# Two attention stages of a whole-model kernel: TensorE's order fixed in the code, with padded last keys

## The chip, the cores and the metric

The kernel runs on one core of a Trainium2 chip. A core has TensorE (PE in the profile: matrix products and transposes; its weight loads are PEld), VectorE (DVE), ScalarE (ACT), GpSimd (POOL) and SyncE (SP, which issues transfers here). Each engine works through a queue of its own, in order; semaphores hold an instruction until what it reads is ready and what it overwrites has been read. The metric is device time in microseconds (us) of one execution. The kernel before takes 2580.34 us, the median of 3 runs (2580.19 to 2582.79).

## The reference

The program computes two whole transformer-like layers in float32 for 512 tokens of width 1024. The change lies in the mixer of the first block, which has 16 extra leading tokens ("meta", 528 in all) and two attentions of 8 heads of 64. Queries are taken in four blocks of 128; a block sees the meta tokens and all blocks up to its own. In the code heads go in pairs, so that there are 4 chunks of heads times 4 query blocks.

```python
def stick_breaking_attention(q, k, v):
    ...
        z = jnp.einsum('bhtd,bhsd->bhts', q[:, :, q0:q1], k[:, :, :q1]).astype(jnp.float32) * scale
        strict = jnp.arange(q1)[None, :] < jnp.arange(q0, q1)[:, None]
        log_1m = jnp.where(strict, jax.nn.log_sigmoid(-z), 0.0)
        csum = jnp.cumsum(log_1m, axis=-1)
        log_a = jax.nn.log_sigmoid(z) + csum[..., -1:] - csum
        a = jnp.where(strict, jnp.exp(log_a), 0.0)
        outs.append(jnp.einsum('bhts,bhsd->bhtd', a.astype(v.dtype), v[:, :, :q1]))
def latent_attention(q_nope, q_rope, k_nope, k_rope, v, cid):
    ...
        s = (jnp.einsum('bhtd,bhsd->bhts', q_nope[:, :, q0:q1], k_nope[:, :, :kend])
             + jnp.einsum('bhtd,bsd->bhts', q_rope[:, :, q0:q1], k_rope[:, :kend]))
        p = jax.nn.softmax(jnp.where(mask, s, NEG_INF), axis=-1)
        outs.append(jnp.einsum('bhts,bhsd->bhtd', p.astype(v.dtype), v[:, :, :kend]))
```

After them come `gate_sb * (y_sb @ w_sb_o) + gate_mla * (y_mla @ w_mla_o)` with sigmoid gates, and `@ w_out`.

## The kernel before

**Long products.** Every weight matrix is loaded in float32 tiles (`wraw`, two buffers), split by ACT into a rounded part `whi` (L286) and by DVE into the rest `wlo` (L287), three buffers each. A projection is then three products for every 128 rows of depth (L301: hi by xh, hi by xl, lo by xh) into a PSUM bank of the pool `l`. A product has 512 columns (`lin1`), or it goes as a pair of 256 and 272 columns into two banks (`lin2`, 528 tokens). In the two attention stages the pools are z=2 (scores), l=2, a=2 (transposes and attention outputs): `l` holds two banks, and whoever writes the third waits for the eviction of the first.

**`stick`, the stick-breaking attention.** For each chunk c: the projections of the next chunk's q (`sbq`, evicted by DVE at L683) and k (`sbk`, evicted in two halves by L247), four of the 16 gate projections (`gs`, `gm`), and for each query block b a short chain: scores on PE (both heads in one tile, L709, for 144 and 272 keys; one head at a time, L669, for 400 and 528), a mask product (L671, L711), on ACT Abs (L226), Exp and Ln (L236), on DVE `sp` (L723), a running sum `cs` (L727), `e` (L731, L733), and on ACT the last Exp. `attn_pv` then transposes the probabilities on PE (L634), copies them out of PSUM (`at`, L638; the last 16 keys, L640) and multiplies them by v (L645), two heads in the two halves of the columns; ACT and DVE store the result (`ysbh`, `ysbl`).

**`latent`, the softmax attention.** First v (`mlav`) is made by 30 long products (L757) of `uv`; then for each chunk q and k (`uq`, `uk`; copies by ACT, L243) and in chunks 0 and 2 the rotated part `t12`, which needs the table `rope` (a DMA at L748). The chain is a maximum on DVE (L800, L802), Exp with its sum on ACT (L236), reciprocal and scaling on DVE (L814, L816), and `attn_pv` as above. The 8 projections by `wo` of the stick result (96 products) stand in the code behind the loop. Behind the stage, `wo` of the latent result is multiplied by the gate on DVE, added to the other half on POOL (`gm`, L609) and split (`ooh`, `ool`) for `wout` (L328).

**What sets the order.** The framework orders the instructions of all engines by priorities and its own cost estimates. `attn_pv` and the weight splits stand in `high_priority(offset=100)`; so a short product goes in when the framework believes it ready, between any two long ones.

Of the kernel before, what the change touches and what calls it, by code (L numbers as in the profile page):

```python
# [215 lines left out]
class Kern:  # L216
# [301 lines left out]
    def mixer(self, n, h):  # L518
# [15 lines left out]
        with ExitStack() as stS:  # L534
            S = self.pool(stS, "S")
            vt = S.tile([P, 5, 512], F32, name="sbv")
            with ExitStack() as st:
# [53 lines left out]
            self.stick(S, x, n.rs, vt, ysb, masks[:, :P], gs, gm)  # L591
# [7 lines left out]
        with ExitStack() as st:  # L599
            self.latent(st, cq, ckv, kr, masks[:, P:], ymla, ysb, gs)  # L600
# [20 lines left out]
    def attn_pv(self, pool, probs, c, nb, vt, ydst, b):  # L621

        nc = self.nc
        hp = ExitStack()
        hp.enter_context(self.tc.high_priority(offset=100))
        slots = [(i, hh) for i in range(nb) for hh in range(2)] + [(nb, hh) for hh in range(2)]
        where = {}
        for g0 in range(0, len(slots), 4):
            grp = slots[g0:g0 + 4]
            pt = self.sbank()  # L630
            at = pool.tile([P, 512], F32, name="at", bufs=3)
            for j, (i, hh) in enumerate(grp):
                kk = P if i < nb else META
                nc.tensor.transpose(pt[:kk, j * P:(j + 1) * P], probs[hh][:, i * P:i * P + kk], self.ident)  # L634
                where[(i, hh)] = at[:kk, j * P:(j + 1) * P]
            n1 = sum(1 for i, hh in grp if i < nb)
            if n1:
                (nc.vector.tensor_copy if (g0 // 4) % 2 else nc.scalar.copy)(at[:, :n1 * P], pt[:, :n1 * P])  # L638
            if n1 < len(grp):
                nc.vector.tensor_copy(at[:META, n1 * P:len(grp) * P], pt[:META, n1 * P:len(grp) * P])  # L640
        po = self.sbank()[:, :P]
        for i in range(nb + 1):
            kk = P if i < nb else META
            for hh in range(2):
                nc.tensor.matmul(po[64 * hh:64 * hh + 64, :], vt[:kk, i, (2 * c + hh) * 64:(2 * c + hh + 1) * 64],  # L645
                                 where[(i, hh)], start=i == 0, stop=i == nb)
        sl = slice(b * P, (b + 1) * P)
        nc.scalar.copy(ydst[0][:, c, sl], po)
        self.tt(ydst[1][:, c, sl], po, ydst[0][:, c, sl], ALU.subtract)
        hp.close()  # L650

    def units(self):

        for b in range(4):
            n = META + (b + 1) * P
            for heads in (((0, 1),) if n <= 272 else ((0,), (1,))):
                z = self.psp["z"].tile([P, 2, 512], F32, name="z", tag="z")
                if n <= 512:
                    yield b, heads, n, z[:, :len(heads), :n], [[(z[:, i, :n], 0, n)] for i in range(len(heads))]
                else:  # L660
                    w = n // 2
                    yield b, heads, n, z[:, :, :w], [[(z[:, s, :w], s * w, (s + 1) * w) for s in range(2)]]

    def scores(self, pieces, q, k, mask):

        nc = self.nc
        for i, (ps, a, b) in enumerate(pieces):
            last = i == len(pieces) - 1
            nc.tensor.matmul(ps, q, k[:, a:b], start=True, stop=not last)  # L669
            if last:  # L670
                nc.tensor.matmul(ps[:, b - a - P:], self.idb, mask, start=False, stop=True)  # L671

    def stick(self, S, x, rs, vt, ysb, mask, gs, gm):
# [3 lines left out]
        qk = {}  # L677

        def proj(c):
            q = S.tile([P, T], F32, name="sbq", bufs=2)  # L680
            k = S.tile([P, TM], F32, name="sbk", bufs=2)
            ps = self.lin1(d["sbq"][c], x, KD, META)
            nc.vector.scalar_tensor_tensor(q, ps, 0.125, rs[:, META:], op0=mul, op1=mul)  # L683
            for p, a, b in self.lin2(d["sbk"][c], x, KD):
                self.tt(k[:, a:b], p, rs[:, a:b], mul)
            qk[c] = q, k

        def gates(i):
            for m in range(4 * i, 4 * i + 4):
                ps = self.lin1(d["gate"][m], x, KD, META)  # L690
                dst = (gs if m < KD else gm)[:, m % KD, :]
                self.tt(dst, ps, rs[:, META:], mul)
                nc.gpsimd.tensor_scalar(dst, dst, self.v("b_gate", m), 1.0, op0=add, op1=mul)

        proj(0)
        late = None
        for c in range(4):
            if c < 3:
                proj(c + 1)
            if c:  # L700
                gates(c - 1)
            q, k = qk[c]
            probs = {}
            for b, heads, n, z, pieces in self.units():
                nh = len(heads)
                if nh == 2:
                    for hh in heads:
                        r = slice(64 * hh, 64 * hh + 64)
# [657 lines left out]
```

## Time and profile before

| | us |
|---|---|
| median of 3 runs | 2580.34 |
| the profiled execution | 2579.18 |
| span of its trace | 2577.4 |
| `stick`, first score to last product by `sbv` | 171.7 (512.1 to 683.8) |
| end of `stick` (last gates) | 693.9 |
| `latent` with its `uv` and `wo`, to the first product of `ymh` | 112.4 (693.9 to 806.3) |

PE is busy for 98% of the span, DVE for 53%, ACT for 38%. The granted clock of TensorE is 0.996 of full speed on the mean. Times in the trace are from the span's start.

### The profile page before, as it was taken

The page shows a single profiled execution, that of the slowest core. Times are in us where ns is not written, and L with a number is a line of the kernel's source. Part 1 is how long each engine was busy: PE and PEld are TensorE (multiplying, and loading weights), DVE is VectorE, ACT ScalarE, POOL GpSimd, SP SyncE. Part 2 cuts the span into 40 slices and gives each one's busy share as a digit, 9 for nine tenths or more (in the row PEclk, how much of TensorE's full clock was granted, in tenths as well). Part 3 has the DMA queues.
Part 4 walks back from the last instruction along what each step waited for, and adds up shares of the span by engine and source line. Part 5 has one row for each costly group of instructions (what it writes and reads, how often), then busy time and mean ns, then how long its engine had stood idle before and what let it go on. Part 6 is the DMA issues. An engine that isn't in the chain of part 4 may idle for free.

```text
span 2577.4 us, 33167 instructions
## 1 busy us (share of the span) xinstructions
PE 2526.4 (98%) x13330; PEld 2087.8 (81%) x13334; DVE 1355.5 (53%) x2108; ACT 978.6 (38%) x1561; POOL 312.2 (12%) x250
## 2 busy tenths in 40 slices
PE   8999999999999999999999999999999899999999
PEld 8999997867767788888777788888888568888887
DVE  4324347355565542334678755355475755535544
ACT  4222234344563532223534633223344553322332
POOL 3101011011102120101100111001122111100110
PEclk9999999999999999999999999999999999999999
DMA  4222333211112423333323332332333213233232
GB/s 137 91 91 84 98 92 132 75 57 58 51 38 81 147 98 98 95 101 100 107 85 98 115 98 92 92 103 96 92 109 99 58 43 129 94 94 100 94 93 98
DMA packets 76339, 239.43 MB, mean 93 GB/s; under 512 B 9044, under 2 KB 11348, under 8 KB 75928
## 3 DMA queue, kind: packets, MB, share of 16 engines
q1 hardware_dynamic: 76184, 237.30, 29.2%
q8 instruction: 105, 1.72, 0.3%
q14 instruction: 50, 0.41, 0.1%
HBM read 225.72 MB, written 8.40 MB: 91 GB/s over the span
## 4 chain that ended last, share of the span: by engine, by line
PE 88%; DVE 5%; ACT 3%; issue 2%; POOL 1%; DMA 1%; SPq 0%; DVEq 0%; POOLq 0%; ACTq 0%
PE l L301 75%; PE l L328 3%; PE a L645 2%; PE z L669 1%; PE l L314 1%; PE a L634 1%; DVE h L247 1%; DVE xl L404 1%; PE s L1272 1%; PE a L382 1%; PE a L1294 0%; POOL gm L247 0%; DVE wlo L287 0%; PE a L1300 0%; ACT whi L286 0%
## 5 line engine op out<-in xcount | busy, mean ns | idle before, releaser
L286 ACT CAST whi<-wraw 128x1024 fp32r<-128x1024 f32 (+4 forms) x440 | 430.3, 979 | 1115.2 <-PE l L301 911.0
L301 PE MATMUL l<-xh,whi 128*128 128x512 f32 (+3 forms) x2368 | 785.5, 357 | 0.5 <-DVE sbk L247 0.5
L301 PE MATMUL l<-xh,wlo 128*128 128x512 f32 (+3 forms) x2368 | 780.9, 356 | 0.0
L301 PE MATMUL l<-xl,whi 128*128 128x512 f32 (+3 forms) x2368 | 780.7, 355 | 0.0
L287 DVE TENSOR_TENSOR wlo<-wraw,whi 128x1024 fp32r<-128x1024 f32 (+4 forms) x440 | 503.4, 1145 | 283.8 <-ACT whi L286 272.7
L301 PEld LDWEIGHTS l<-xh,whi 128*128 128x128 f32 (+1 forms) x2368 | 421.3, 188 | 66.1 <-issue 4.8
L301 PEld LDWEIGHTS l<-xh,wlo 128*128 128x128 f32 (+1 forms) x2368 | 420.7, 188 | 63.7 <-issue 1.9
L301 PEld LDWEIGHTS l<-xl,whi 128*128 128x128 f32 (+1 forms) x2368 | 421.5, 188 | 62.3 <-issue 2.1
L247 POOL TENSOR_TENSOR acc<-acc,sq 128x512 f32<-128x512 f32 (+1 forms) x63 | 99.9, 1586 | 471.1 <-ACT sq L226 434.2
L301 PE MATMUL l<-chh,whi 128*128 128x512 f32 x384 | 149.4, 389 | 0.0
L301 PE MATMUL l<-chl,whi 128*128 128x512 f32 x384 | 149.4, 389 | 0.0
L301 PE MATMUL l<-chh,wlo 128*128 128x512 f32 x384 | 149.4, 389 | 0.0
L247 POOL TENSOR_TENSOR t<-g,xrs 128x528 f32<-128x528 f32 (+1 forms) x44 | 75.8, 1724 | 563.8 <-ACT g L236 563.8
L301 PE MATMUL l<-hh,wlo 128*128 128x256 f32 (+2 forms) x528 | 140.1, 320 | 0.0
L301 PE MATMUL l<-hh,whi 128*128 128x256 f32 (+2 forms) x528 | 140.0, 319 | 0.0
L301 PE MATMUL l<-hl,whi 128*128 128x256 f32 (+2 forms) x528 | 139.8, 319 | 0.0
L247 POOL TENSOR_TENSOR cc<-cc,xrs 128x512 f32<-128x512 f32 x48 | 62.8, 1308 | 586.7 <-ACT cc L236 586.7
L247 DVE TENSOR_TENSOR t<-l,t 128x256 f32<-128x256 f32 (+1 forms) x66 | 32.3, 516 | 148.1 <-PE l L301 144.8
L247 DVE TENSOR_TENSOR g<-l,xrs 128x256 f32<-128x256 f32 (+1 forms) x66 | 32.3, 516 | 122.2 <-PE l L301 116.2
L301 PEld LDWEIGHTS l<-hh,whi 128*128 128x128 f32 x528 | 88.3, 188 | 6.9
L301 PEld LDWEIGHTS l<-hh,wlo 128*128 128x128 f32 x528 | 88.1, 188 | 6.9
L301 PEld LDWEIGHTS l<-hl,whi 128*128 128x128 f32 x528 | 88.1, 188 | 6.8
(342 smaller groups left out, 3202.9 us busy)
## 6 DMA issues: line engine op xcount, KB each, us to landing
wraw<-in_up SPq DMA_DIRECT2D x96, 512.0 KB, 3.4
wraw<-in_dn SPq DMA_DIRECT2D x64, 384.0 KB, 3.1
wraw<-in_ffn_g SPq DMA_DIRECT2D x44, 512.0 KB, 3.4
wraw<-in_ffn_u SPq DMA_DIRECT2D x44, 512.0 KB, 3.4
wraw<-in_ffn_d SPq DMA_DIRECT2D x32, 448.0 KB, 3.3
wraw<-in_hy SPq DMA_DIRECT2D x20, 512.0 KB, 3.4
wraw<-in_ffn_d SPq DMA_DIRECT2D x16, 512.0 KB, 3.5
wraw<-in_gate SPq DMA_DIRECT2D x16, 512.0 KB, 3.4
```

What stands on the lines that cost most here:

```text
L247: return (eng or self.nc.vector).tensor_tensor(out, a, b, op=op)
L286: nc.scalar.copy(hi, raw)
L287: nc.vector.tensor_tensor(lo, raw, hi, op=ALU.subtract)
L301: self.nc.tensor.matmul(ps, a[:, k * m:(k + 1) * m], b[:, k0 + k, c0:c1], start=first and k == 0 and pi == 0, stop=last and k == kc - 1 an ...
L314: self.nc.tensor.matmul(ps[:c1 - c0, :n], a[:, k, c0:c1], b[:, j * n:(j + 1) * n], start=k == 0 and pi == 0, stop=k == nk - 1 and pi == 2)
L328: self.nc.tensor.matmul(ps, a[:, k * P:(k + 1) * P], b[:, k, t0:t1], start=k == 0 and pi == 0, stop=k == kc - 1 and pi == 2)
L382: nc.tensor.matmul(p[:, c - a:c - a + w], r[:w, i:i + 1].to_broadcast([w, P]), self.ident[:w, :w], start=True, stop=True)
L404: nc.vector.scalar_tensor_tensor(n.x[1][:, k, :], hs[k], g, n.x[0][:, k, :], op0=ALU.mult, op1=ALU.subtract)
L634: nc.tensor.transpose(pt[:kk, j * P:(j + 1) * P], probs[hh][:, i * P:i * P + kk], self.ident)
L645: nc.tensor.matmul(po[64 * hh:64 * hh + 64, :], vt[:kk, i, (2 * c + hh) * 64:(2 * c + hh + 1) * 64], where[(i, hh)], start=i == 0, stop=i ...
L669: nc.tensor.matmul(ps, q, k[:, a:b], start=True, stop=not last)
L1272: nc.tensor.matmul(z[:, i * n:(i + 1) * n], qt[r, 2 * g + i, b * P:(b + 1) * P], kt[r, g, k0:k0 + n], start=False, stop=i == 1)
```

## The change

In both stages PE's order is now the order of the code (`by_hand`). A projection is a generator that yields after each step (a 512-column product, or a 256+272 pair), and `fill(n)` puts n steps between the short groups. The other engines are still ordered by the framework.

- `attn_pv` is split into `attn_t` (transposes, copies) and `attn_v` (the products by v, now one unbroken group of a block). The last 16 keys are copied into a `rest` tile of 128 rows whose other rows are zero, and v's last block is zeroed too, so that their product has 128 rows.
- The scores of the two heads of 400 and 528 keys are issued beside each other.
- Gates are spread 3, 4, 4, 5 over the chunks of `stick` (before: none, 4, 4, 4 and 4 behind the loop).
- In `latent`, `uq` and `uk` of chunk 0 stand ahead of the `uv` products, and `wo` of the stick result is spread 2, 1, 2, 3 over the chunks.
- Behind `latent`, the addition of `gm` and `gs` goes to DVE for m of 5 and more.

```diff
+    def by_hand(self):
+        return self.tc.manual_schedule(engines={mybir.EngineType.PE})
+    def step_lin(self, src, x, kc, done, c0=0, two=False):
+        hi, lo = self.wload(src, kc * P)
+        segs, ev = self.banks2() if two else self.banks1(c0)
+        for k in range(kc):
+            for pi, (a, b) in enumerate(((hi, x[0]), (hi, x[1]), (lo, x[0]))):
+                for ps, t0, t1 in segs:
+                    self.nc.tensor.matmul(ps, a[:, k * P:(k + 1) * P], b[:, k, t0:t1],
+                                          start=k == 0 and pi == 0, stop=k == kc - 1 and pi == 2)
+                yield
+        done(ev)
+    def fill(self, steps=None):
+        n = 0
+        while self.todo and (steps is None or n < steps):
+            if next(self.todo[0], self) is self:
+                self.todo.pop(0)
+            else:
+                n += 1
...
-            self.tt(gm[:, m, :], gm[:, m, :], gs[:, m, :], add, nc.gpsimd)
+            self.tt(gm[:, m, :], gm[:, m, :], gs[:, m, :], add, nc.gpsimd if m < 5 else None)
...
+    def last_keys(self, pt, o, probs, nb, rest, where):
+        for hh in range(2):
+            self.nc.tensor.transpose(pt[:META, o + hh * P:o + (hh + 1) * P], probs[hh][:, nb * P:nb * P + META], self.ident)
+            where[(nb, hh)] = rest[:, hh * P:(hh + 1) * P]
+        self.nc.vector.tensor_copy(rest[:META, :], pt[:META, o:o + 2 * P])
+    def attn_v(self, where, c, nb, vt, ydst, b):
...
+            po = self.sbank()[:, :P]
+            for i in range(nb + 1):
+                for hh in range(2):
+                    nc.tensor.matmul(po[64 * hh:64 * hh + 64, :], vt[:, i, (2 * c + hh) * 64:(2 * c + hh + 1) * 64],
+                                     where[(i, hh)], start=i == 0, stop=i == nb)
...
+    def scores(self, units, q, k, mask):
...
+        for row in zip(*todo):
+            for hh, (ps, a, b), last in row:
+                nc.tensor.matmul(ps, q(hh), k(hh)[:, a:b], start=True, stop=not last)
...
+            def qdone(ev):
+                nc.vector.scalar_tensor_tensor(q, ev[0][0], 0.125, rs[:, META:], op0=mul, op1=mul)
+            def kdone(ev):
+                for p, s in ev:
+                    self.tt(s(k), p, s(rs), mul)
+            yield from self.step_lin(d["sbq"][c], x, KD, qdone, META)
+            yield from self.step_lin(d["sbk"][c], x, KD, kdone, two=True)
...
+        for c in range(4):
+            ng = (3, 4, 4, 5)[c]
+            self.todo = ([proj(c + 1)] if c < 3 else []) + [gates.pop(0) for _ in range(ng)]
+            if c == 0:
+                self.fill(8)
+            probs = start(c, 0)
+            if late:
+                self.attn_v(*late)
+            self.fill(12)
+            for b in range(4):
+                if b < 3:
+                    nxt = start(c, b + 1)
+                    self.fill((14, 18, 22)[b])
+                else:
+                    self.fill(24 * ng + (48 if c < 3 else 0) - (8 if c == 0 else 0) - 102)
+                t = self.attn_t(S, probs, c, b + 1, vt, ysb, b, rest[b % 2])
+                self.fill(6)
+                if b < 3:
+                    self.attn_v(*t)
+                    self.fill(4)
+                    probs = nxt
+                else:
+                    late = t
+            self.fill()
+        self.attn_v(*late)
...
+        self.todo = [proj(0)]
+        self.fill()
+        w = self.wload(d["uv"][0], 1024)
...
+        late, m = None, 0
+        for c in range(4):
+            nm = (2, 1, 2, 3)[c]
+            self.todo = ([proj(c + 1)] if c < 3 else []) + [wo(m + i) for i in range(nm)]
+            m += nm
+            probs = start(c, 0)
+            if late:
+                self.attn_v(*late)
+            self.fill(6)
+            for b in range(4):
+                if b < 3:
+                    nxt = start(c, b + 1)
+                    self.fill(5)
+                t = self.attn_t(L, probs, c, b + 1, vt, ymla, b, rest[b % 2])
+                self.fill(4)
...
```

How the order moves, at three places. On PE in chunk 2 of `stick`, the products by v of the last block of chunk 1 (`sbv`) stand in the program before singly between long products:

```order
L301 MATMUL l<-xl,whi 128x512
L301 MATMUL l<-xh,wlo 128x512
L645 MATMUL a<-at,sbv 64x128
L301 MATMUL l<-xh,whi 128x512
L645 MATMUL a<-at,sbv 64x128
L301 MATMUL l<-xl,whi 128x512
L645 MATMUL a<-at,sbv 64x128
L301 MATMUL l<-xh,wlo 128x512
```

and in the changed one, at a block's end, together (`rest` is the padded tile):

```order
L712 MATMUL z<-masks,idb 128x128
L683 MATMUL a<-at,sbv 64x128 x8
L683 MATMUL a<-rest_4908,sbv 64x128 x2
L343 MATMUL l<-xh,whi 128x512
L343 MATMUL l<-xl,whi 128x512
```

Ten products by v stand in one group where they stood one by one between long ones.

On DVE, the evictions of the projections `sbq` and `sbk` of chunk 2 stand before between single operations of the block of 528 keys:

```order
L733 SCALAR_TENSOR_TENSOR e<-z,cs 128x528
L287 TENSOR_TENSOR wlo<-wraw,whi 128x1024
L683 SCALAR_TENSOR_TENSOR sbq<-l,xrs 128x512
L723 SCALAR_TENSOR_TENSOR sp<-z,e 128x528
L247 TENSOR_TENSOR sbk<-l,xrs 128x256
L727 SCALAR_TENSOR_TENSOR cs<-cst,sp 128x528
L733 SCALAR_TENSOR_TENSOR e<-z,cs 128x528
L247 TENSOR_TENSOR sbk<-l,xrs 128x272
```

and in the changed program, in chunk 1, behind the whole chain of the 272-key block and of the 400-key block:

```order
L762 SCALAR_TENSOR_TENSOR sp<-z,e 128x544
L766 SCALAR_TENSOR_TENSOR cs<-cst,sp 128x272 x2
L770 SCALAR_TENSOR_TENSOR e<-z,cs 128x272 x2
L734 SCALAR_TENSOR_TENSOR sbq<-l,xrs 128x512
L287 TENSOR_TENSOR wlo<-wraw,whi 128x1024
L674 COPY rest_4907<-a 16x256
L247 TENSOR_TENSOR ysbl<-a,ysbh 128x128
L762 SCALAR_TENSOR_TENSOR sp<-z,e 128x400 x2
L766 SCALAR_TENSOR_TENSOR cs<-cst,sp 128x400 x2
L772 SCALAR_TENSOR_TENSOR e<-z,cs 128x400 x2
L287 TENSOR_TENSOR wlo<-wraw,whi 128x1024
L247 TENSOR_TENSOR sbk<-l,xrs 128x256
```

Each eviction has moved from the middle of a chain to its end.

On ACT, the copies of q and k of the second chunk of `latent` stand before ahead of the Exps of the first two blocks (128x144, 128x272):

```order
L243 COPY q_6730<-l 64x512
L243 COPY q_6733<-l 64x512
L243 COPY k_6756<-l 64x256
L243 COPY k_6760<-l 64x256
L286 CAST whi<-wraw 128x384
L243 COPY k_6756<-l 64x272
L243 COPY k_6760<-l 64x272
L236 ACTIVATE e,sm<-z,sm 128x144 x2
L236 ACTIVATE e,sm<-z,sm 128x272 x2
```

and in the changed program behind them:

```order
L236 ACTIVATE e,sm<-z,sm 128x144 x2
L286 CAST whi<-wraw 128x512
L236 ACTIVATE e,sm<-z,sm 128x272 x2
L243 COPY q_6766<-l 64x512
L243 COPY q_6769<-l 64x512
L665 COPY at<-a 128x256
L286 CAST whi<-wraw 128x384
L243 COPY k_6807<-l 64x256
L243 COPY k_6807<-l 64x272
```

The copies have moved behind four Exps, and go head by head instead of half by half.

## Rows read from the trace of the kernel before

**Rows 1.** The page, part 1: engine, busy us, share of span, instructions.

```profile
PE 2526.4 (98%) x13330; PEld 2087.8 (81%) x13334; DVE 1355.5 (53%) x2108; ACT 978.6 (38%) x1561; POOL 312.2 (12%) x250
```

**Rows 2.** Busy time in two stretches (`latent`, `stick`), with clock, DMA share, GB/s.

```profile
693.90:806.30 112.40, 110.28 (x696) 78.50 (x695) 69.41 (x188) 63.40 (x160) 0.93 (x1) 1.00 0.14 41
512.10:683.80 171.70, 171.25 (x933) 117.83 (x934) 105.61 (x168) 82.43 (x149) 23.85 (x42) 1.00 0.16 54
```

**Rows 3.** What PE waited for, 495 to 807: total, times, longest.

```profile
PE l L301 <- ACT q L243: 1.3, 2, 0.7
```

**Rows 4.** Timeline of PE: start, duration, engine, line, operation; records (two a product).

```profile
545.57 0.43 PE L645 MATMUL a<-at,sbv 128*64 128x128 f32 x2
545.93 0.50 PE L301 MATMUL l<-xh,whi 128*128 128x512 f32 x1
546.37 0.43 PE L645 MATMUL a<-at,sbv 128*64 128x128 f32 x2
```

**Rows 5.** Timeline of PE, ten products by v in one group.

```profile
645.54 0.48 PE L301 MATMUL l<-xh,whi 128*128 128x512 f32 x1
645.95 1.46 PE L645 MATMUL a<-at,sbv 128*64 128x128 f32 x20
647.34 0.50 PE L301 MATMUL l<-xl,whi 128*128 128x512 f32 x1
647.68 0.39 PE L301 MATMUL l<-xh,wlo 128*128 128x512 f32 x1
647.91 0.39 PE L301 MATMUL l<-xh,whi 128*128 128x512 f32 x1
```

**Rows 6.** Timeline of PE, scores of two heads together and of one head.

```profile
656.99 0.73 PE L709 MATMUL z<-sbk,sbq 64*128 64x272 f32 x4
657.65 0.28 PE L711 MATMUL z<-masks,idb 128*128 128x128 bf16 x2
...
664.59 0.94 PE L669 MATMUL z<-sbk,sbq 64*128 64x400 f32 x2
665.46 0.23 PE L671 MATMUL z<-masks,idb 128*128 128x128 bf16 x1
```

**Rows 7.** Timeline of all engines: first and last of a 272-key chain.

```profile
658.42 0.61 ACT L226 ACTIVATE e<-z 128x544 f32<-128x544 f32 x1
...
663.19 0.48 DVE L731 SCALAR_TENSOR_TENSOR e<-z,cs 128x272 f32<-128x272 f32 x1
```

**Rows 8.** DVE by shape, 512 to 684: count, busy us, mean ns, idle before.

```profile
L287 DVE TENSOR_TENSOR wlo<-wraw,whi 128x1024 fp32r<-128x1024 f32 x19 | 23.6, 1244 | 5.1 <-ACT whi L286 5.0
...
L727 DVE TENSOR_TENSOR_SCAN cs<-cst,sp 128x400 f32<-128x400 f32 x8 | 7.9, 986 | 0.1
...
L733 DVE SCALAR_TENSOR_TENSOR e<-z,cs 128x400 f32<-128x400 f32 x8 | 5.1, 634 | 0.5
L723 DVE SCALAR_TENSOR_TENSOR sp<-z,e 128x400 f32<-128x400 f32 x8 | 4.6, 574 | 4.9 <-ACT e L236 4.9
...
L683 DVE SCALAR_TENSOR_TENSOR sbq<-l,xrs 128x512 f32<-128x512 f32 x2 | 1.4, 685 | 0.0
```

**Rows 9.** ACT by shape, 512 to 684.

```profile
L236 ACT ACTIVATE e<-e 128x400 f32<-128x400 f32 x24 | 12.3, 534 | 0.3
```

**Rows 10.** ACT by shape, 693 to 807.

```profile
L243 ACT COPY q<-l 64x512 f32<-64x512 f32 x8 | 4.6, 580 | 0.2 <-PE l L301 0.2
...
L236 ACT ACTIVATE e<-z,sm 128x272 f32<-128x272 f32 x8 | 3.8, 482 | 3.4 <-DVE sm L803 3.4
```

**Rows 11.** Transfers issued 688 to 696: count, KB, us from issue to landing.

```profile
rope<-in_rope SPq DMA_DIRECT2D x1, 528.0 KB, 3.6
```

**Rows 12.** Timeline of PE behind `latent`; in brackets, idle before and releaser.

```profile
835.74 0.78 PE L328 MATMUL l<-ooh,whi 128*128 128x512 f32 x1 [2.09 <-ACT ooh L291]
```

**Rows 13.** Timeline of POOL, the addition behind `latent`.

```profile
832.93 2.11 POOL L247 TENSOR_TENSOR gm<-gm,gs 128x512 f32<-128x512 f32 x1 [2.12 <-DVE gm L247]
```

**Rows 14.** Busy time right behind that wait of PE (columns of rows 2).

```profile
835.78:839.20 3.42, 3.42 (x8) 2.39 (x9) 2.36 (x3) 0.85 (x1) 2.11 (x1) 0.50 0.47 188
```

More of the change, by code (lines that the diff above doesn't have):

```diff
@@ L619, in mixer, with attn_t @@
         return h, upd
-    def attn_pv(self, pool, probs, c, nb, vt, ydst, b):
+    def attn_t(self, pool, probs, c, nb, vt, ydst, b, rest):
         nc = self.nc
-        hp = ExitStack()
-        hp.enter_context(self.tc.high_priority(offset=100))
-        slots = [(i, hh) for i in range(nb) for hh in range(2)] + [(nb, hh) for hh in range(2)]
+        slots = [(i, hh) for i in range(nb) for hh in range(2)]
         where = {}
[L628 to L662, printed above, removed]
@@ L664, in scores @@
-    def scores(self, pieces, q, k, mask):
-        nc = self.nc
[L667 to L671, printed above, removed]
+        with self.tc.high_priority(offset=100):
+            for g0 in range(0, len(slots), 4):
+                grp = slots[g0:g0 + 4]
+                pt = self.sbank()
+                at = pool.tile([P, 512], F32, name="at", bufs=3)
+                for j, (i, hh) in enumerate(grp):
+                    nc.tensor.transpose(pt[:, j * P:(j + 1) * P], probs[hh][:, i * P:(i + 1) * P], self.ident)
+                    where[(i, hh)] = at[:, j * P:(j + 1) * P]
+                n1 = len(grp) * P
+                if n1 <= 256:
+                    self.last_keys(pt, 256, probs, nb, rest, where)
+                (nc.vector.tensor_copy if (g0 // 4) % 2 else nc.scalar.copy)(at[:, :n1], pt[:, :n1])
+            if nb % 2 == 0:
+                self.last_keys(self.sbank(), 0, probs, nb, rest, where)
@@ L673, in stick, with rest_tiles @@
+    def rest_tiles(self, pool):
+        tiles = [pool.tile([P, 2 * P], F32, name=f"rest{i}") for i in range(2)]
+        for t in tiles:
+            self.nc.gpsimd.memset(t, 0.0)
+        return tiles
     def stick(self, S, x, rs, vt, ysb, mask, gs, gm):
@@ L735, in stick, with start @@
                 self.act(e, e, AF.Exp)
-                if heads[-1] == 1:
-                    if late:
-                        self.attn_pv(*late)
-                    late = (S, dict(probs), c, b + 1, vt, ysb, b)
-        self.attn_pv(*late)
-        gates(3)
+            return probs
+        def start(c, b):
+            q, k = qk[c]
+            rows = lambda hh: slice(64 * hh, 64 * hh + 64)
+            units = list(self.units(b))
+            self.scores(units, lambda hh: q[rows(hh), b * P:(b + 1) * P], lambda hh: k[rows(hh), :], mask)
+            return chain(units)
+        self.todo = [proj(0)]
+        self.fill()
+        gates = [gate(m) for m in range(2 * KD)]
+        late = None
+        for c in range(4):
[19 more added lines that the diff above has]
+                    probs = nxt
+                else:
+                    late = t
+            self.fill()
+        self.attn_v(*late)
     def latent(self, st, cq, ckv, kr, mask, ymla, ysb, gs):
@@ L750, in latent @@
         vt = L.tile([P, 5, 512], F32, name="mlav")
[L751 to L759 removed]
+        rest = self.rest_tiles(L)
@@ L792, in latent, with chain @@
+        def chain(units):
             probs = {}
-            for b, heads, n, z, pieces in self.units():
+            for heads, n, z, pieces in units:
                 nh = len(heads)
-                for i, hh in enumerate(heads):
-                    self.scores(pieces[i], qk[hh][0][:, b * P:(b + 1) * P], qk[hh][1], mask)
                 e = L.tile([P, 544], F32, name="e", bufs=4)[:, :nh * n]
```

155 lines of the change are left out of this document (84 added, 71 removed).

## The prediction

> **What bounds the kernel now.** I read the page's busy shares first, then PE's waits in the two stages, then PE's timeline there, then the durations on DVE and ACT. PE is busy for 98% of the span and DVE for about half [rows 1]; in the two stages it is busy for 171.25 of 171.70 us and for 110.28 of 112.40 us at full clock [rows 2], and its largest wait there is 1.3 us in all [rows 3]. So the end is set by how PE's time is used. A 512-column product follows another by .23 us (647.68 to 647.91) [rows 5]. With a product by v before it and one behind it takes far more: from one lone product by v to the next it is .80 us with one long product between [rows 4], so a lone product by v costs .80 - .23 = .57. Ten of them in one group, from the long product before (645.54) to the second behind (647.68), take 2.14 us, less two long products 1.68, .17 each [rows 5]. Going in and out costs (.41 - .23) + (.34 - .23) = .29, call it .3 a group. PE has no slack to hide that, but it has almost no waits to be shortened either: what a rigid order saves on PE is repaid wherever it makes PE wait for DVE or ACT.
>
> **What the change takes away on PE (matmuls equal in number).** The counts are from the program's order, the prices from rows.
> - Twenty lone products by v in `stick` become parts of groups: 20 x (.57 - .17) = 8.0 us.
> - Its 39 groups of products by v become 16; 20 of the 39 are the lone ones, so 3 groups go beside them, and the 2 groups of lone products become whole: 5 x .3 = 1.5.
> - Scores: both heads of 272 keys together take .66 us up to the mask, one head of 400 keys .87 [rows 6]. By columns two heads of 272 apart would take 2 x .87 x 272/400 = 1.18, so together they cost .56 of that. For 400 keys this saves .44 x 1.74 = .77, for 528 keys .44 x 2.30 = 1.01; four chunks: 7.1.
> - Transposes gathered (42 groups to 17), last keys with 128 rows in place of 16: the rows show no price of either alone. Bounds: -1 (zeroed rows cost transfers of nothing on PE, but memsets and a copy in another tile) to 6 (a switch saved, at a quarter of .3 for 25 groups, and .1 for each of 32 blocks' last keys, as estimates). I take 3, near the middle, since a lone operation between long ones was seen only to cost.
> - `latent`: 28 groups of products by v become 16, 12 x .3 = 3.6; its scores are over 96 rows and can't lie beside each other. With padding and the 1.3 us of [rows 3] 0 to 9; I take 5.
> Sum -24.6, call it -25.
>
> The Trainium skill, "TensorEngine Tiling (Array Packing)", Key Properties, says that a change of tiling mode drains the engine; that is the price of .3 a group seen here, and by it alone the change is a pure gain (rival A).
>
> **What it adds: waits.** PE's queue is in order, `l` has two banks. Whatever step needs a third bank stands, with all behind it, till the eviction of an earlier one. The evictions are not ordered by hand.
> - *E1, `sbk` behind `sbq`, chunks 1 and 2.* The scores of the 272-key block are followed by the last 12 steps of `sbq`, then by pairs of `sbk`; `sbk`'s first half takes the one free bank, the second needs that of `sbq`, and `sbq` is evicted on DVE behind the whole chain of that block. From the first Abs to the end of `e` that chain took 663.67 - 658.42 = 5.25 us [rows 7], with a foreign copy of about .4 in it; 4.9, and .69 for the eviction [rows 8]: 5.6. PE has 12 x .23 = 2.8. Wait 2.8, twice: 5.6.
> - *E2, the first gate behind `sbk`, chunks 1 and 2.* `sbk` ends 12 pairs after the scores of 400 keys, 12 x .24 = 2.9 (by columns, 528/512 x .23). Its eviction stands behind that chain and a `wlo`: six ACT passes of .53 [rows 9] and the second `sp` .57, then two scans 1.97, two `e` 1.27, `wlo` 1.24 [rows 8], and about .4 for the half eviction: 3.2 + .6 + 2.0 + 1.3 + 1.2 + .4 = 8.7. Wait 5.8; some of the passes start before the last score ends, so 5.5, twice: 11.
> In chunk 0 eight steps stand ahead of the first scores, and by DVE's order the evictions come before the chains: nothing. Chunk 3 has no projection.
> - *Small ones in `stick`.* The fixed steps between transposes and products by v (6 steps, 1.4 us) have to cover the copy out of PSUM on an engine that is in a chain; for 16 blocks, and for the banks after E1 and E2. The rows don't show it: 0 to 8, I take 4.4, as of a passing operation of .5 at half of 16 blocks. `stick`: 21.
> - *E3, the start of `latent`.* `rope` takes 3.6 us from issue [rows 11], and its place in memory is that of `stick`'s tiles. Before, 30 products by `uv` (30 x .23 = 6.9 us) stood between; now `uq` comes first and its third projection needs a bank that waits for `rope` and its .69. With at most 15 steps (3.5) left: 1 to 3 us, I take 2.5. Then `uk`'s second half waits for two copies of q, and `uv` for copies of k (.58 each or less [rows 10]): 2 x 1.25. Sum 5.
> - *E4, chunks of `latent`.* The copies of q stand on ACT behind the Exps of two blocks. Two Exps .96, two copies 1.16 [rows 10], and about 1 for the maximum ahead of them: 3.1; PE has three long products and half a pair, .8: 2.3 to 2.7 in chunks 0 and 2; in chunk 1 the turned parts come first, 1. Then `wo` waits for copies of k, now head by head: .9 to 1.6, three times. Sum 2.7 + 1.1 + 2.7 + 3.6 = 10, and some 2 at blocks' ends: 12. `latent`: 17.
> New waits 38. Of them DVE and ACT make up nothing: the chains themselves start from PE.
>
> **The clock.** A wait of 2.09 us [rows 12] was followed by 3.4 us at granted clock .50, that is 1.2 of 2.4 GHz, with 8 products in it [rows 14], where .23 would have room for 15: 7 x .23 = 1.6 us lost. E1, E2, E3 and two of E4 are seven waits longer than that; not each must be followed by a drop. Five of seven: 8 us; bounds 0 and 11.
>
> Against the change also speaks the Trainium skill, "TensorE: Matmul & The Clock Gate", A second HAM failure mode: waiting in short bits between groups for PSUM can make the clock swing. The trace disagrees for short waits: the stage with those of [rows 3] kept 1.00 [rows 2]. By the rule the small waits too would cost, and the time would go towards 2613, the end of rival E; by the rows they don't, and the sum goes by these.
>
> **Behind `latent`.** The addition on POOL, 2.11 us [rows 13], stands in the way to PE's 2.09 wait [rows 12]; on DVE the like takes .69 [rows 8]. The wait and its drop, 2.1 + 1.6, mostly go, -2.5; bounds 0 and -3.7.
>
> **Sum.** -25 + 38 + 8 - 2.5 = +18.5 from the profiled execution, 2579.18: 2597.7. The median stands 1.2 above it, but the small terms are the least sure and PE may use up some of them; 2597 for the median.
>
> **Rivals.**
> A. *No new waits decide.* If DVE's and ACT's evictions come in time (their queues have slack, 53% and 38% busy [rows 1], and the same order was kept with 1.3 us of waits [rows 3]), only the savings count: 2580 - 25 - 2.5 = 2553, or 2565 if a third of the waits stay. Against it: the order of DVE's rows itself; an eviction can't overtake a chain in its queue. Chance 17%.
> B. *The waits come, the clock holds.* 2580 - 25 + 38 - 2.5 = 2590. For it: the idle periods are near the one that was followed by a drop. 22%.
> C. *Break-even.* The small waits of `stick`, E3 and E4 are half as long (38 - 10.7), no drops: 2580 - 25 + 27 - 2.5 = 2580. 8%.
> D. *My forecast,* waits with four to seven drops: 2593 to 2602. 40%.
> E. *More waits than counted* (each block's copies late by .5 to 1 for both stages, 32 x .5 = 16 more): 2613. 13%.
> The change could also fail to do what it says, if the order on PE weren't that of the code; it is, but for a few products of `uq` that move ahead.
>
> Faster by over 0.2% (5.2 us, about what a measurement of this kernel can tell from no change) is A and a little of C: 0.20. Within: most of C, 0.08. Slower: 0.72. The range that leaves out 2 in 10 cuts the far halves of A and E: 2565 to 2612; the likeliest case's own is 2588 to 2606.
>
> **What would show it.** In the changed profile, PE's waits on `sbq` and `sbk` evictions by DVE: two each of about 2.8 and 5.5, none in chunks 0 and 3; on ACT's q and k copies in `latent`, some 10 us; one on `rope`. `stick` from first score to last product by `sbv` (the gates inside are spread otherwise, so long products must be counted) would carry 20 less in short work. Stretches of 3.4 us at .50 behind the long waits. No lone product by v; scores of 400 keys in pairs at about 1 us. The forecast is wrong if the two stages show under 15 us of waits (then A), or if the saving in short work is far from 25.

## The result and the profile after

The changed kernel takes 2594.24 us (median of 5, 2590.99 to 2600.2) against 2580.34 (median of 5); the ratio is 1.0055, with a 95% interval of 1.0042 to 1.0068. It is slower by 14 us, 0.5%; the interval lies above 1. The forecast was 2597.

The profiled execution took 2595.59 us with a span of 2593.7. The page's first part, after, against [rows 1]:

```profile
PE 2511.8 (97%) x13330; PEld 2095.6 (81%) x13334; DVE 1354.1 (52%) x2111; ACT 976.9 (38%) x1561; POOL 307.3 (12%) x253
```

PE runs as many matmuls as before in 14.6 us less busy time, and the span is 16.3 us longer: PE waits. What it waited for between 490 and 870 us (the seven largest: total, times, longest), against [rows 3]:

```profile
PE l L343 <- DVE sbk L247: 10.1, 4, 4.6
PE l L343 <- ACT q L243: 7.3, 4, 2.5
PE l L343 <- DVE sbq L734: 6.7, 4, 2.7
PE l L343 <- ACT k L243: 3.3, 3, 1.4
PE l L343 <- ACT sl L236: 2.2, 1, 2.2
PE a L672 <- ACT at L665: 1.6, 6, 0.3
PE l L328 <- DVE wlo L287: 1.5, 1, 1.5
```

All but the last two lines are long products (L343) that wait for a bank of `l`. The name behind the arrow is the eviction that frees the bank, but for `sl`, which stands for a wait for `rope` (shown further down). Before, the largest entry of the two stages was 1.3.

**The first kind of wait, in rows.** PE's timeline in chunk 1 of `stick` (start, duration, in brackets the idle time before and its releaser):

```profile
553.90 0.28 PE L343 MATMUL l<-xh,whi 128*128 128x256 f32 x1
556.86 0.40 PE L343 MATMUL l<-xh,whi 128*128 128x272 f32 x1 [2.68 <-DVE sbq L734]
```

The half with 256 columns got a bank, the half with 272 stood for 2.68 us. DVE's timeline of that time says why:

```profile
553.30 0.73 DVE L762 SCALAR_TENSOR_TENSOR sp<-z,e 128x544 f32<-128x544 f32 x1 [3.79 <-ACT e L236]
554.07 1.34 DVE L766 TENSOR_TENSOR_SCAN cs<-cst,sp 128x272 f32<-128x272 f32 x2
555.32 0.88 DVE L770 SCALAR_TENSOR_TENSOR e<-z,cs 128x272 f32<-128x272 f32 x2
556.12 0.68 DVE L734 SCALAR_TENSOR_TENSOR sbq<-l,xrs 128x512 f32<-128x512 f32 x1
556.72 1.21 DVE L287 TENSOR_TENSOR wlo<-wraw,whi 128x1024 fp32r<-128x1024 f32 x1
```

The eviction of `sbq` had nothing to wait for when `sbq`'s last product had run; it stood behind the three operations of the 272-key chain. The second kind, PE and then DVE, where the chain of 400 keys and a `wlo` stand ahead of `sbk`:

```profile
566.33 0.41 PE L343 MATMUL l<-xh,wlo 128*128 128x256 f32 x2
571.37 0.74 PE L343 MATMUL l<-xh,whi 128*128 128x512 f32 x1 [4.64 <-DVE sbk L247]
```

```profile
565.95 1.06 DVE L762 SCALAR_TENSOR_TENSOR sp<-z,e 128x400 f32<-128x400 f32 x2 [3.81 <-ACT e L236]
566.92 1.87 DVE L766 TENSOR_TENSOR_SCAN cs<-cst,sp 128x400 f32<-128x400 f32 x2
568.70 1.15 DVE L772 SCALAR_TENSOR_TENSOR e<-z,cs 128x400 f32<-128x400 f32 x2
569.76 1.22 DVE L287 TENSOR_TENSOR wlo<-wraw,whi 128x1024 fp32r<-128x1024 f32 x1
570.90 0.76 DVE L247 TENSOR_TENSOR sbk<-l,xrs 128x256 f32<-128x256 f32 x2
```

DVE itself had been idle for 3.81 us before that chain: it is not short of time, it is short of freedom in its order. Both waits come again in chunk 2 with the same lengths. The long product behind the wait took .74 in place of .39: the clock. A stretch behind the first wait (busy time of PE, PEld, DVE, ACT, POOL, then the granted clock), to be read beside [rows 14]:

```profile
557.80:561.21 3.41, 3.41 (x20) 3.17 (x20) 0.55 (x2) 0.37 (x1) 0.00 (x0) 0.50 0.51 159
```

Five such stretches lie in the two stages (558, 571, 626, 711, 780 us), none behind `latent`, where before had its one.

**What the short work costs now.** PE's timeline, the scores of two heads of 400 keys and a group of ten products by v:

```profile
562.59 0.94 PE L709 MATMUL z<-sbk,sbq 64*128 64x400 f32 x4
563.47 0.28 PE L712 MATMUL z<-masks,idb 128*128 128x128 bf16 x2
...
602.68 1.09 PE L683 MATMUL a<-at,sbv 128*64 128x128 f32 x16
603.60 0.39 PE L683 MATMUL a<-rest,sbv 128*64 128x128 f32 x4
603.92 0.50 PE L343 MATMUL l<-xh,whi 128*128 128x512 f32 x1
```

Two heads take .88 up to their masks, as one head did before [rows 6]: the second is free. The ten products by v take 1.24 from first to next long product, where the group of [rows 5] took 1.39.

**Where the time went, closed.** From the last product that makes `sbv` to the last product of `wout` by `ooh`, each trace's length less PE's idle periods over .12 us (summed over its timeline) less 1.6 us for each 3.4 us at clock .50 gives the work that PE did there:

| run | length | waits | half-clock stretches | work |
|---|---|---|---|---|
| before | 388.8 | 5.7 | 1 | 381.5 |
| after | 400.2 | 36.5 | 5 | 355.7 |
| x1 evictions early | 390.0 | 26.0 | 5 | 356.0 |
| x2 eight steps first | 384.2 | 24.9 | 2 | 356.1 |
| x3 no hand order | 387.8 | 15.4 | 5 | 364.4 |
| x4 uv first | 402.5 | 34.6 | 8 | 355.1 |
| x5 halves in turn | 368.1 | 13.5 | 0 | 354.6 |
| x6 all of them | 364.3 | 10.4 | 0 | 353.9 |
| x7 heads in turn | 420.9 | 36.5 | 10 | 368.4 |
| x8 last keys of 16 rows | 405.4 | 35.9 | 6 | 359.9 |
| x9 halves, no hand order | 372.7 | 8.8 | 1 | 362.4 |
| x10 before, halves in turn | 387.2 | 6.3 | 0 | 380.9 |
| x11 halves, gm on POOL | 374.5 | 14.6 | 3 | 355.1 |

The change took 25.8 us of work away and added 30.8 of waits and 4 x 1.6 of clock: 11.4 us more in this stretch. The seven runs with the changed short work in the hand order (after, x1, x2, x4 to x6, x11) have 354 to 356 us of work with waits from 10 to 36 and 0 to 8 stretches; the price of 1.6 fits all of them. The rest of the profiled span, outside the changed stages, took 2577.4 - 388.8 = 2188.6 us before and 2593.7 - 400.2 = 2193.5 after: 4.9 more, with seven half-clock stretches where before had five (without the span's last 4 us). So of the 16.3 us by which this span grew, the changed stretch explains 11.4.

### The profile page after: what moved, and what is told of

Same layout as the page of the kernel before. It is cut to its first block, busy times and chain, and to the rows that moved or that the text cites. A ratio compares the mean times of both kernels' runs of the same rounds, so it can differ in the third digit from the quotient of the medians.

```text
span 2593.7 us, 33187 instructions
## 1 busy us (share of the span) xinstructions
PE 2511.8 (97%) x13330; PEld 2095.6 (81%) x13334; DVE 1354.1 (52%) x2111; ACT 976.9 (38%) x1561; POOL 307.3 (12%) x253
## 4 chain that ended last, share of the span: by engine, by line
PE 84%; DVE 6%; issue 4%; ACT 4%; POOL 1%; DMA 1%; SPq 0%; DVEq 0%; ACTq 0%; POOLq 0%
PE l L301 68%; PE l L343 5%; PE l L328 3%; PE l L314 1%; PE z L709 1%; PE a L683 1%; DVE h L247 1%; DVE wlo L287 1%; DVE xl L429 1%; ACT e L236 1%; ACT whi L286 1%; PE a L407 1%; PE s L1371 1%; PE a L392 0%; POOL acc L247 0%
## 5 line engine op out<-in xcount | busy, mean ns | idle before, releaser
L301 PE MATMUL l<-xh,whi 128*128 128x512 f32 (+3 forms) x2144 | 704.5, 356 | 0.0
L301 PE MATMUL l<-xh,wlo 128*128 128x512 f32 (+3 forms) x2144 | 701.4, 354 | 0.0
L301 PE MATMUL l<-xl,whi 128*128 128x512 f32 (+3 forms) x2144 | 701.3, 354 | 0.0
L301 PEld LDWEIGHTS l<-xh,whi 128*128 128x128 f32 (+1 forms) x2144 | 381.0, 188 | 56.3 <-issue 1.3
L301 PEld LDWEIGHTS l<-xl,whi 128*128 128x128 f32 (+1 forms) x2144 | 380.8, 188 | 55.8 <-issue 0.8
L301 PEld LDWEIGHTS l<-xh,wlo 128*128 128x128 f32 (+1 forms) x2144 | 380.5, 188 | 55.5 <-issue 0.3
L343 PE MATMUL l<-xh,whi 128*128 128x512 f32 (+1 forms) x224 | 80.7, 381 | 16.8 <-DVE sbk L247 10.1
```

Of the source, the lines that this page charges most:

```text
L301: self.nc.tensor.matmul(ps, a[:, k * m:(k + 1) * m], b[:, k0 + k, c0:c1], start=first and k == 0 and pi == 0, stop=last and k == kc - 1 an ...
L343: self.nc.tensor.matmul(ps, a[:, k * P:(k + 1) * P], b[:, k, t0:t1], start=k == 0 and pi == 0, stop=k == kc - 1 and pi == 2)
```

## The experiments

Theory Q: PE's steps wait for banks whose evictions stand behind a chain in DVE's or ACT's queue. Rivals: the saving isn't real, or the waits only move. Ratios are to the kernel before as timed beside each run, with 95% intervals, since its median moved between 2576.6 and 2580.3.

**x1, evictions early.**

```diff
             def qdone(ev):
-                nc.vector.scalar_tensor_tensor(q, ev[0][0], 0.125, rs[:, META:], op0=mul, op1=mul)
+                with self.tc.high_priority(offset=100):
+                    nc.vector.scalar_tensor_tensor(q, ev[0][0], 0.125, rs[:, META:], op0=mul, op1=mul)
```

and the same in `kdone`.

> The changed kernel, with the evictions of sbq and sbk in high priority; PE's order is the same. In DVE's order of chunks 1 and 2 the eviction of sbq moves ahead of one scan (.71 us) and both e (.48 each), that of sbk ahead of both scans of 400 keys (.99 each), both e (.63 each) and a wlo (1.24). Theory Q (the loss is PE waiting for evictions that stand behind chains in DVE's queue): the waits of 2.68 become about 1.0 and those of 4.64 about .2, 2 x (1.7 + 4.4) = 12 us less, and three or four of the clock drops there go (1.6 us each): 17 to 19 us less than the changed kernel, about 2576. Rival P (PE's short work did not get cheaper in the fixed order, the waits only fill what would be lost anyhow): within 4 us of the changed kernel, 2590 to 2598. Rival M (the waits only move, to transposes that wait for the delayed e): 5 to 8 us less, about 2588.

2579.22 us, ratio 1.0002 (.9994 to 1.0011). PE's order is that of after, only a few operations of DVE and ACT changed places, and some 14 us are gone. The waits of 2.68 are 1.25, those of 4.64 are .65, as PE's waits from 490 to 700 show:

```profile
PE l L343 <- DVE sbq L735: 3.8, 4, 1.3
PE l L343 <- DVE sbk L247: 2.2, 4, 0.7
```

Rival P falls, and no new wait of M's size appears. Of the 12 us of waits 10.5 went (36.5 to 26.0 in the table). The stretches at half clock stayed at five in this trace, all in `latent`: the 5 to 7 us for the clock did not come in it.

**x2, eight steps first.**

```diff
-            if c == 0:
-                self.fill(8)
+            self.fill(8)
...
-                    self.fill(24 * ng + (48 if c < 3 else 0) - (8 if c == 0 else 0) - 102)
+                    self.fill(24 * ng + (48 if c < 3 else 0) - 8 - 102)
```

> The changed kernel, with eight steps ahead of the first scores in all four chunks (in the changed one only in chunk 0), taken off the steps ahead of the last transposes. Theory Q: chunks 1 and 2 get what chunk 0 has, where evictions stand ahead of the chains: waits of 2.68 and 4.64 fall to about .4 each, 2 x 6.5 = 13 us less, and three or four clock drops of 1.6 us: 18 us less than the changed kernel, about 2576. Rival P: no change, 2590 to 2598. Rival M: waits appear at the last block of each chunk, which has eight steps fewer ahead of it, 8 steps x .23 x 4 = up to 7 us: about 2583.

2574.92 us, ratio .9989 (.998 to .9998). As expected of theory Q, and Q alone. PE's waits from 490 to 700:

```profile
PE l L343 <- DVE t L247: 3.4, 1, 3.4
PE l L343 <- DVE sbq L734: 2.7, 4, 0.7
PE l L343 <- DVE sbk L247: 1.7, 4, 0.5
```

Four waits of .7 and four of about .4 are left, about what the evictions themselves take (.68 and .38 in the rows above). No new wait appears at the last blocks (rival M falls), though the start of `latent` got 3.4 in this trace.

**x3, no hand order.**

```diff
     def by_hand(self):
-        return self.tc.manual_schedule(engines={mybir.EngineType.PE})
+        return ExitStack()
```

> The changed kernel, with the framework ordering PE too (padded last keys, heads beside each other, gates and wo spread in the code's order, products by v issued as one block all stay). On PE the products by v form 39 groups in the two stages (67 before, 32 in the changed one), none with single products. Theory Q: the cheaper short work stays nearly whole and the waits are mostly filled by other steps: 25 us saved less about .3 x 7 groups, less some 10 us of waits in place of 35, no more than two drops in these stages: 2580 - 23 + 10 + 2 - 2 = about 2567 to 2572, faster than both kernels. Rival H (the saving comes from the fixed order itself; the framework's order makes it as dear as before): 2578 to 2582.

2577.22 us, ratio .9995 (.9986 to 1.0005): no gain over before, where 8 to 13 were expected. Work fell by 17.1 us (381.5 to 364.4), so groups, pairs and padding do work without the hand order, but waits and clock took it back. The largest wait, PE and then DVE:

```profile
562.81 1.12 PE L709 MATMUL z<-sbk,sbq 64*128 64x264 f32 x4 [2.73 <-DVE e L772]
```

```profile
562.06 1.15 DVE L772 SCALAR_TENSOR_TENSOR e<-z,cs 128x400 f32<-128x400 f32 x2
```

The scores of 528 keys stand for a bank of `z` that the chain before still reads; twice 2.73 us, and each was followed by two stretches at .50. That the framework believed the chain done sooner is likely, but not shown. I had expected the free order to fill such holes; it didn't fill these two. It too is fixed when the program is built.

**x4, uv first.** The block of `uv` products moved back ahead of `self.todo = [proj(0)]` in `latent`.

> The changed kernel, with the 30 products by uv ahead of the projections of latent's first chunk, as in the kernel before. Theory Q: rope and the copies of q land behind 6.9 us of long products: of the waits of 2.23, 1.32 and 1.30 us at 705 to 712 the first goes and with it one clock drop of 1.6; uv's own wait for a bank (.58 before) comes back, and the copies of k must be waited for by the first scores: 3 us less than the changed kernel, about 2591. Rival (the waits are only passed on to the first scores of latent): no change, 2594.

2592.05 us, ratio 1.0058 (1.0045 to 1.0071), the same as after. The waits fell by 1.9 us only: 2.23, 1.32 and 1.30 went, and .49, .53, 1.23 and .85 came, at uv's banks, at `uk`'s second half and at the first scores. Eight half-clock stretches lie in this trace, six of them in `stick`, where after has three with the same program and the same waits. The rival is nearer: the place of `uv` is worth little.

**x5, halves in turn.**

```diff
-        for k in range(kc):
-            for pi, (a, b) in enumerate(((hi, x[0]), (hi, x[1]), (lo, x[0]))):
-                for ps, t0, t1 in segs:
+        n = 0
+        for ps, t0, t1 in segs:
+            for k in range(kc):
+                for pi, (a, b) in enumerate(((hi, x[0]), (hi, x[1]), (lo, x[0]))):
                     self.nc.tensor.matmul(ps, a[:, k * P:(k + 1) * P], b[:, k, t0:t1],
                                           start=k == 0 and pi == 0, stop=k == kc - 1 and pi == 2)
-                yield
+                    n += 1
+                    if n % len(segs) == 0:
+                        yield
```

> The changed kernel, with the two halves of a 528-column projection one after the other (24 products of 256 columns, then 24 of 272) in place of pairs; a step is still two products, and all steps stay where they are. So only one bank is needed at a time: the second half needs the bank of sbq 2.8 us later, and the first gate that of the first half. Theory Q (two banks and late evictions): the waits of 2.68 and 4.64 in chunks 1 and 2 go, 14.7 us, the .67 + .48 + .67 + .39 of the first projections too, 2.2, and three or four clock drops of 1.6: 22 us less than the changed kernel, about 2572, faster than before by some 7. Rival W (weights loaded for products of 256 columns in a row are no longer hidden behind a pair's second): 96 steps of sbk and 24 of uk at up to .07 more, 8 us back: 2580. Rival P (no wait decides): 2590 to 2598.

2555.78 us, ratio .9918 (.9904 to .9932): 21 us faster than before, some 35 faster than after. No wait of `stick` over .25 us is left. PE's waits from 490 to 700, and its timeline where the first half ends, the second begins and the first gate follows:

```profile
PE l L344 <- ACT q L243: 2.4, 2, 1.7
PE l L344 <- ACT sl L236: 2.3, 1, 2.3
PE a L686 <- ACT at L668: 1.0, 5, 0.2
```

```profile
549.50 0.28 PE L344 MATMUL l<-xh,wlo 128*128 128x256 f32 x1
549.71 0.94 PE L712 MATMUL z<-sbk,sbq 64*128 64x400 f32 x4
550.59 0.28 PE L715 MATMUL z<-masks,idb 128*128 128x128 bf16 x2
550.68 0.37 PE L344 MATMUL l<-xh,whi 128*128 128x272 f32 x1
...
553.66 0.29 PE L344 MATMUL l<-xh,wlo 128*128 128x272 f32 x1
553.79 0.40 PE L344 MATMUL l<-xh,whi 128*128 128x512 f32 x1
```

A projection now needs one bank at a time, so an eviction has a whole half, 24 products or about 3 us, to come late. The products cost what they did in pairs (.12 and .13 apart; work 354.6): rival W falls. More came than the 22 expected. In the table the stretch is 32 us shorter than after's: 23 of waits where 17 were expected, since `uk` in `latent` is such a pair too (the waits for copies of q and k fell from 11.9 to 4.8), 8 of clock, with no stretch at .50 left, and 1 of work. Another 10 us of the profiled spans' difference lie outside: this execution, the fastest of six, has a granted clock of 1.000 on the mean.

**x6, all together:** x5 with each half evicted as it ends, x2, x4, and q's and k's copies in high priority, half by half.

> The changed kernel, with all of it: halves in turn and each half evicted when it is done, eight steps first in every chunk, the products by uv first in latent, the copies of q and k on ACT in high priority and k half by half. Theory Q: of the changed kernel's 36.5 us of waits between 490 and 870 some 10 stay (uv's banks 1.8, q's copies about 2, transposes and tails 5), and none of its five clock drops there but one: 26 + 6 = 32 us less, about 2562 to 2566, faster than before by 13 to 17. Rival: ACT and DVE fall behind in their chains when evictions go first, and new waits of 10 us appear at transposes: 2574.

2556.13 us, ratio .9915 (.9901 to .9929), the same as x5 within the interval, though its stretch is 3.8 us shorter (364.3), with 10.4 us of waits, as expected. The time doesn't show it because the rest of its profiled span is 7.8 us longer than x5's (2191.5 against 2183.7), with eight half-clock stretches outside the two stages where x5's execution has none but at the span's end. At like clock x6 is faster: its executions at .997 took 2553.67 and 2554.21 us, those of x5 at .998 took 2557.09 and 2557.36. So the rest still takes some 4 us off. x5 and x6 are the fastest; x9 and x11 below beat both kernels too.

**x7, heads in turn.**

```diff
-        for row in zip(*todo):
-            for hh, (ps, a, b), last in row:
-                nc.tensor.matmul(ps, q(hh), k(hh)[:, a:b], start=True, stop=not last)
         for row in todo:
-            hh, (ps, a, b), _ = row[-1]
+            for hh, (ps, a, b), last in row:
+                nc.tensor.matmul(ps, q(hh), k(hh)[:, a:b], start=True, stop=not last)
             nc.tensor.matmul(ps[:, b - a - P:], self.idb, mask, start=False, stop=True)
```

> The changed kernel, with the scores (and mask) of the second head behind those of the first for all blocks. By the prediction's term for scores: 400 keys .77 and 528 keys 1.01 more a chunk, and 144 and 272 keys, paired before too, .3 and .5: 2.6 x 4 = 10 us more, about 2604. A part of it may fall into waits that are there (E1 and E2 begin at the scores' end, so they move along): then the whole 10 still counts. Rival: pairing gives nothing on PE, since two products by 64 rows run one after the other in any order: within 2 us of the changed kernel.

2610.75 us, ratio 1.0126 (1.0113 to 1.0139). The work is 12.7 us more than after's, and its waits the same 36.5; the rest of the time is five more stretches at half clock. In PE's timeline the two heads of 400 keys:

```profile
561.78 0.94 PE L709 MATMUL z<-sbk,sbq 64*128 64x400 f32 x2
562.65 0.23 PE L710 MATMUL z<-masks,idb 128*128 128x128 bf16 x1
562.81 0.94 PE L709 MATMUL z<-sbk,sbq 64*128 64x400 f32 x2
563.68 0.23 PE L710 MATMUL z<-masks,idb 128*128 128x128 bf16 x1
563.72 0.49 PE L343 MATMUL l<-xh,whi 128*128 128x256 f32 x2
```

1.94 us from first score to next long product, where after has .97 (562.59 to 563.56). Pairing halves a block's scores; the rival falls.

**x8, last keys of 16 rows.**

```diff
+                    kk = P if i < nb else META
-                    nc.tensor.matmul(po[64 * hh:64 * hh + 64, :], vt[:, i, (2 * c + hh) * 64:(2 * c + hh + 1) * 64],
-                                     where[(i, hh)], start=i == 0, stop=i == nb)
+                    nc.tensor.matmul(po[64 * hh:64 * hh + 64, :], vt[:kk, i, (2 * c + hh) * 64:(2 * c + hh + 1) * 64],
+                                     where[(i, hh)][:kk], start=i == 0, stop=i == nb)
```

> The changed kernel, with the last keys' products by v over 16 rows, as before (the rest tile and its copy stay; only the rows that the product reads are fewer). By the estimate of .1 for each of 32 blocks: 3 us more, 2597. Rival Z (a product's time goes by its columns, 16 or 128 rows are the same): no change, within 1.5 us of the changed kernel.

2596.34 us, ratio 1.0067 (1.0055 to 1.0079): by the time alone it can't be told from after. By the trace it can: 4.2 us more work, and the same group of ten now takes 1.39 (598.78 to 600.17) in place of 1.24:

```profile
598.78 1.09 PE L684 MATMUL a<-at,sbv 128*64 128x128 f32 x16
599.81 0.43 PE L684 MATMUL a<-rest,sbv 16*64 16x128 f32 x4
600.17 0.50 PE L343 MATMUL l<-xh,whi 128*128 128x512 f32 x1
```

.15 a block, .10 of it before the first 16-row product; 32 blocks give 4.8.

**x9, halves without hand order; x10, before with halves.** x9 is x5 with x3's edit; x10 lets `lin2` of before call `mm` once for each half.

> The changed kernel with the halves in turn (x5), and the framework ordering PE too (x3). Between the last product that makes sbv and the last of wout, x3 had 364.4 us of work without waits and clock drops, the hand-ordered runs 354 to 356. Theory Q: the halves in turn take the bank waits away here too, but x3's 2.7 us waits of scores for a z bank (behind e on DVE) and the 8.7 us of dearer short work (39 groups of products by v in place of 32) stay: 2577 - 4 - 2 = about 2570, 14 slower than x5. Rival (with banks free the order by hand is worth nothing): 2556 to 2560.

> The kernel before, with the halves of a 528-column projection in turn (six places use it, two in the stages). Theory Q: before had 5.7 us of waits in that stretch, of which .5 and 1.3 for banks of halves, so 0 to 2 us less: 2575 to 2578, the same within noise. Rival (halves in turn are cheaper on PE by themselves): 5 us less or more, 2571.

x9 took 2563.61 us, ratio .994 (.9926 to .9955); x10 2579.25, ratio 1.0002 (.9993 to 1.001). So halves in turn are worth nothing in the kernel before, which hardly waits for such banks. In the changed code they are worth some 35 us with the order by hand (x5 against after) and some 14 without it (x9 against x3). Over them, the hand order is worth 7.8 us of work (362.4 to 354.6) and 6 to 8 in time (the ratios, the medians). x9 lies between Q's 2570 and the rival's 2556 to 2560: z's waits of 2.73 went too, which I had expected to stay. Why they went was not tested.

**x11, gm on POOL:** x5 with `nc.gpsimd` for all m.

> x5 with the addition of gm and gs back on POOL for all m. By the prediction's term: a wait of 2.1 in place of 1.5 before wout and a clock drop of 1.6: 2 us more than x5, 2558. Rival (the end of that stage is set by wlo and the split, not by the addition): within 1 us of x5.

2564.8 us (2559.1 to 2573.56), ratio .9947 (.9925 to .9968), 9 more than x5, not 2. The tail is as expected, PE's wait before `wout` being .6 longer than the 1.51 of x5 and followed by a stretch at half clock:

```profile
821.02 0.49 PE L328 MATMUL l<-ooh,whi 128*128 128x512 f32 x1 [2.10 <-ACT ooh L291]
```

Together with a wait of .77 that x5 lacks, that is 1.4 + 1.6 = 3.0 us. Two more stretches at .50 lie in `latent`, which this edit doesn't touch, and five outside the two stages, where the profiled execution of x5 had none. At like clock the edit costs what I expected: at .998 x11 took 2559.1 and 2559.75 us and x5 2557.09 and 2557.36; at .995 x11 took 2564.26 and 2565.34 and x5 2564.35. So of the 9 us about 2 or less are the edit's, and the rest goes with the clock of the other executions (below).

## Why the prediction was right

- *The saving, -25.* Measured 25.8 as work. Its parts shared it otherwise than I had put it: the scores save more, since the second head is free (.97 for two heads against 1.94; x7 gives 12.7 for all pairs, where the paired blocks of before are among them), padding is worth 4 to 5 (x8), where I had put 3 for it and the gathered transposes together. The price of a pair was mis-sized: I took .56 of two single heads by columns, it is .50. What the lone products by v, the fewer groups and `latent` gave was not measured apart; by what is left it was somewhat less than I had put.
- *E1, 2.8 twice:* 2.68 twice. *E2, 5.5 twice:* 4.64 twice; I let the chain of 8.7 us begin at the scores' end, while it begins at their start (562.59, evicted 571.3). x1 and x2 show that these were evictions behind chains; no rival explains that moving an eviction, or the step by eight, takes away the wait.
- *Small waits of `stick`, 4.4:* 3.4, but in the main from elsewhere: 2.2 are waits for the evictions of `sbq` and `sbk` of the first two projections (.67, .48, .67, .39), the last two of them in chunk 0, where I had put nothing; the copies out of PSUM took 1.2. That the sum is near is luck. *E3, 5:* 4.9, and its first wait, put down to ACT's `sl`, is `rope`'s: DVE's row beside it names it.

```profile
704.41 0.69 DVE L247 TENSOR_TENSOR t<-l,rope 128x512 f32<-128x512 f32 x1 [2.66 <-DMA rope<-in_rope]
```

- *E4, 12:* 2.46 + .85 + 1.15 + 1.39 + 2.40 + 1.02 = 9.3, and 2.7 at blocks' ends.
- *The clock, five drops, 8 us:* five in this execution; the number is not the program's alone, as x4's six in the same `stick` against three show. *Behind `latent`, -2.5:* PE's waits there went from 2.09 + .78 to 1.50 + .15 and its drop is gone, -2.8. x11 gives 3.0 the other way.
- *The sum.* The waits without the tail come to 34.9 where before had 2.8: 32 more, where I had 38. With the other terms as measured that is -25.8 + 32 + 8 - 2.8 = 11.4 in the changed stretch, where my sum says 18.5. The profiled execution is 16.4 longer than before's, as another 4.9 us came outside the stretch, with more half clock there, for which the prediction has no term. The mechanism and its parts were right; that 2597 came within 3 us of the median is in part luck.
- Rival A failed on the point named against it, the order in DVE's queue; x5, which keeps the order on PE and takes the need for the bank away, is close to A's case, at 2556 where A said 2553. Rival B (the clock holds) is wrong for this kernel in these traces.

## What to carry to other kernels

An order fixed on one engine is only as good as the order of the engines that must free its buffers: read, for each step that needs a buffer, which instruction frees it and what stands ahead of that in its queue. Where a step needs two buffers at once out of two, make it need one at a time before touching any priority; here that was worth some 35 us, x1's priorities 14. Judge such a change by work, waits and clock apart, and compare times at like clock: here 26 us of good work was hidden under 31 us of waits and 6 of clock.

## What the runs showed of the hardware

- The same wait is followed by half clock in one execution and not in another. In x5 and x11 `latent` has the same program and the same wait of 1.69 us for q's copy; the stretch behind it in x5, and then in x11 (columns as above, the granted clock before the last two):

```profile
696.50:699.92 3.42, 3.40 (x22) 2.36 (x23) 0.85 (x2) 2.16 (x6) 0.00 (x0) 1.00 0.12 26
```

```profile
699.27:702.68 3.41, 3.41 (x13) 1.97 (x10) 0.85 (x2) 1.33 (x4) 0.00 (x0) 0.50 0.17 58
```

The after trace itself has two waits of 2.68, one followed by half clock and one not. And the wait of 2.09 behind `latent` from which the prediction took its price [rows 12] comes again in x10, with the clock held, to be read beside [rows 14]:

```profile
838.64 0.49 PE L328 MATMUL l<-ooh,whi 128*128 128x512 f32 x1 [2.09 <-ACT ooh L291]
```

```profile
838.68:842.10 3.42, 3.19 (x13) 2.42 (x14) 2.37 (x3) 0.86 (x1) 2.11 (x1) 1.00 0.43 168
```

In or right behind all six waits of 4.6 us in the traces (two each in after, x4 and x8) half clock began. The Trainium skill, "TensorE: Matmul & The Clock Gate", What's actually happening, calls the number of products at the slow clock at a kernel's start run-variable; the rows here are of waits in mid-kernel, where it varies whether a stretch comes at all, and no row here counts the products at a start.
- The mean granted clock of an execution goes with its time. x5's six go from 2553.67 us at 1.000 to 2564.35 at .995, x11's six from 2559.1 at .998 to 2573.56 at .990, and the kernel before, one program, was timed from 2572.85 at 1.000 to 2586.64 at .994. Differences of some us between medians of six can be that alone.
- Two products by 64 rows each, in the two halves of the rows, take the time of one (.88 in after against .87 in before and x7, for 400 columns).
- The first product by 16 rows behind products by 128 rows starts .10 us later than one by 128 rows does there (x8 against after, same group), though it has less to do.
